# Weight rings whose four slots begin at different bytes modulo 256, in a decoder layer on one core

## Chip, cores and metric

The kernel runs on one core of a Trainium2 chip. The metric is the device time of one execution in microseconds (us); the median of three runs counts.

## What is computed

One step of a hybrid decoder layer for 264 tokens at once: 256 of a prompt and 8 samples, each with model width D = 2048. Everything is float32. Cut to its products, the reference is

```
z  = rms_norm(x) @ w_in                     # 2048 -> 3584: pool, lru, lru gate, conformer a, b
y_pool = pool_mixer(z_pool)  @ w_pool_br    # 512  -> 2048
y_lru  = (rg_lru(conv(z_lru)) * gelu(z_gate)) @ w_lru_br   # 1024 -> 2048
y_conf = silu(layer_norm(conv31(a * sigmoid(b)))) @ w_conf_br   # 512 -> 2048
gates  = sigmoid(rms_norm(x) @ w_gate + b_gate)            # 2048 -> 3 x 2048
x = x + (g_a * y_pool + g_b * y_lru + g_c * y_conf) @ w_out
x = x + square(relu(rms_norm(x) @ w_up)) @ w_down          # 2048 -> 8192 -> 2048
y = rms_norm(x)
```

The new recurrent states (the last rows of the convolutions and the pooling window, and the last h) are outputs too.

## The kernel before, in words

**Three matmuls for one product.** A float32 number is split into a high part, rounded to the type float32r, and a low part, the rest. For each tile of 128 x 128 weights `mm3` (lines 193 to 196) issues three matmuls: high weights by high x (L194), high weights by low x (L195), low weights by high x (L196). The weights are the operand that is loaded into the array; x is the moving operand, 264 columns wide (N = 264). So each matmul has a weight load of its own, which the profile lists as PEld.

**Chunks.** `weight_plan` cuts all weights into 478 chunks of 128 partitions x 1024 floats. A dense chunk holds two k-tiles (kt = 0, 1; 128 rows of the weight matrix each) of 512 output columns, so four tiles of 128 columns (m = 0 to 3) for each k-tile: 2 x 4 x 3 = 24 matmuls. A group is one block of 512 output columns: its chunks, numbered c, run over the rows of the matrix, and its four sums lie in four PSUM tiles. There are 472 dense chunks. Four chunks of lru gate weights stand between those of w_in, and behind chunk 3 of the first w_gate group stand one of group weights of the pooling ("grp") and an empty one. All the chunks are numbered i in the order of the work. Most groups have 8 chunks (16 k-tiles), those of w_lru_br 4, those of w_pool_br and w_conf_br 2.

**Rings.** Three rings of buffers carry the chunks. `raw` has NRAW = 6 slots of 1024 floats, filled by DMA from SyncE's queue (`dma_pair`, L138 for a pair of chunks in one transfer of 1 MB, or `dma_part`, L146 for one chunk). `split(j)` (L177, L178) turns a raw chunk into its two parts: ScalarE (ACT) casts to `whi`, VectorE (DVE) subtracts and writes `wlo`. These two have NHI = 4 slots; chunk j goes to slot j % 4. In the main loop, step i issues the split of chunk i + 3 (AHEAD), at even i the transfer of chunks i + 8 and i + 9, and then the matmuls of chunk i. Pairs from chunk SINGLE on are transferred as one.

**The moving operand.** Tiles of shape [128, ..., 264] in float32r hold x: `A` (high in k-tiles 0 to 15, low in 16 to 31), `xn` for w_up, `LH` and `Q` for the branches and the second half of the hidden layer, `L` for the lru gates. K-tile k of a chunk c is 2c + kt; one k-tile of x is 264 floats, 1056 bytes in each partition.

**Places in SBUF.** Tiles are placed one after the other in the order in which they are declared, behind the DMA scratch at byte 0 of each partition: raw, whi, wlo, qtmp, X, A, four tiles of 8 x 264 (tmp0 to tmp3, later xn), L, G, par, st, rstd, ones, ones_r and small ones. A tile that is declared later under the same tag takes the place of the earlier (Q that of qtmp, LH that of L). whi and wlo begin at byte 128 modulo 256.

**The other work.** Normalisation, convolutions, the scan, gates and splits of x run on ACT, DVE and GpSimd (POOL) between the splits, by a planner that has a budget for each engine and step (`run_bg`). At step 140 POOL issues the store of the states `st` (L973). Single matmuls with a tile of ones sum over the partitions for the norms (`ones_mm`, L271, and L992 at the end). The lru gates take twelve matmuls for one chunk, six for each of two k-tiles of L (`lru_gate_mm`).

The matmuls of one dense chunk are

```
for kt in range(2):
    for m in range(4):
        s = slice(kt * 512 + m * P, kt * 512 + (m + 1) * P)
        xh, xl = rhs(2 * c + kt)
        mm3(pss[m], whi[:, i % NHI, s], wlo[:, i % NHI, s], xh, xl, c == 0 and kt == 0, stop)
```

except for the first four chunks, where the three products go round the four m in turn, and the last two, where m is the outer loop.

Of the kernel before, what the change touches and what calls it, by code (L numbers as in the profile page):

```python
# [10 lines left out]
F32R = mybir.dt.float32r  # L11
# [4 lines left out]
P = 128  # L16
# [30 lines left out]
CH = 1024  # L47
NRAW = 6
NHI = 4
LRU_AT = ((4, 1), (4, 3), (4, 5), (4, 6))  # L50
WARM = 17
LEAD = 4
SINGLE = 18
AHEAD = 3


# [5 lines left out]
def weight_plan():  # L62
# [14 lines left out]
    for gi, (name, _, k, m) in enumerate(groups):  # L77
        for c in range(k // 2):
            chunks.append(("dense", gi, c, CH))
            if name == "w_in" and (m, c) in LRU_AT:  # L80
                chunks.append(("lru", LRU_AT.index((m, c)), 0, 512))
            if (name, m) == ("w_gate", 0) and c == 3:
# [5 lines left out]
def hybrid_step(ctx: ExitStack, tc: tile.TileContext, first, par_in, st_in, wall, y_out, st_out):  # L88
    nc = tc.nc
    cpool = ctx.enter_context(tc.tile_pool(name="cpool", bufs=1))  # L90
# [5 lines left out]


    raw = cpool.tile([P, NRAW, CH], F32, name="raw")
    whi = cpool.tile([P, NHI, CH], F32R, name="whi")
    wlo = cpool.tile([P, NHI, CH], F32R, name="wlo")  # L100
    qtmp = cpool.tile([P, 16 * N], F32, name="qtmp", tag="Q")
    X = cpool.tile([P, KD, N], F32, name="X")
    A = cpool.tile([P, 32, N], F32R, name="A")
# [4 lines left out]
    st = cpool.tile([P, S_OUT], F32, name="st")  # L108
# [7 lines left out]
    def pv(name, i=None, n=1):  # L116
        a, b = PCOL[name]
        return par[:, a:b] if i is None else par[:, a + i:a + i + n]

    def acc():  # L120
        return psum.tile([P, 512], F32, name="acc", tag="acc")
# [11 lines left out]
    def dma_pair(p):  # L133
        s = (2 * p) % NRAW
        if p >= n_pairs:
            return
        if 2 * p >= SINGLE and chunks[2 * p][3] == chunks[2 * p + 1][3] == CH:
            nc.sync.dma_start(raw[:, s:s + 2, :], wall[p - FIRST // 2].rearrange("p (a c) -> p a c", a=2))  # L138
        else:
            for h in range(2):  # L140
                if chunks[2 * p + h][3]:
                    dma_part(2 * p + h, 0, chunks[2 * p + h][3])
# [27 lines left out]
    def split(j, half=None):  # L170
        if j >= len(chunks) or not chunks[j][3]:
            return
        r, h, lo = raw[:, j % NRAW, :], whi[:, j % NHI, :], wlo[:, j % NHI, :]
        s = slice(0, chunks[j][3])
        if half is not None:
            s = slice(half * 512, half * 512 + 512)
        nc.scalar.copy(h[:, s], r[:, s])  # L177
        nc.vector.tensor_tensor(lo[:, s], r[:, s], f(h[:, s]), op=ALU.subtract)  # L178
# [133 lines left out]
    def x_tile(k):  # L312
        x_high(k)
        x_low(k)
# [31 lines left out]
    def softplus():  # L346
        sc = G[:, 8, :]
        t0, t1, t2, w, t4 = (sc[:, 8 * i:8 * i + 8] for i in range(5))
        lam = pv("lru_lambda")
        nc.scalar.activation(t0, lam, AF.Abs)  # L350
        nc.scalar.activation(w, t0, AF.Exp, scale=-1.0)
        nc.vector.tensor_scalar(t0, w, 2.0, None, op0=ALU.add)
        nc.vector.reciprocal(t1, t0)
        nc.vector.tensor_scalar(t4, lam, -1.0, 0.0, op0=ALU.mult, op1=ALU.max)
        eng = nc.gpsimd
        eng.tensor_tensor(t0, w, t1, op=ALU.mult)
        eng.tensor_tensor(t1, t0, t0, op=ALU.mult)
        terms = 10
        eng.memset(t2, 2.0 / (2 * terms + 1))
        for i in range(terms - 1, -1, -1):  # L360
            eng.tensor_tensor(t2, t2, t1, op=ALU.mult)
            eng.tensor_scalar(t2, t2, 1.0, 2.0 / (2 * i + 1), op0=ALU.mult, op1=ALU.add)
        eng.tensor_tensor(t2, t2, t0, op=ALU.mult)
        eng.tensor_tensor(t2, t2, t4, op=ALU.add)
        eng.tensor_scalar(sp[:, 0:8], t2, 4.0, 0.0, op0=ALU.mult, op1=ALU.add)
        eng.tensor_scalar(sp[:, 8:16], t2, -8.0, 0.0, op0=ALU.mult, op1=ALU.add)
# [89 lines left out]
    def lru_gate_mm(ct, c, j):  # L456
        assert "xc" in done
        hi, lo = whi[:, c % NHI, :], wlo[:, c % NHI, :]
        out = []
# [248 lines left out]
    def grp_mm(c):  # L708
        assert "pool" in done
        hi, lo = whi[:, c % NHI, :], wlo[:, c % NHI, :]  # L710
        for gi in range(4):
# [137 lines left out]
    def group(gi):  # L849
        name, k0, _, m = groups[gi]  # L850
        if name == "w_in":
            def rhs(i):
                return A[:, i, :], A[:, 16 + i, :]
            fn = {0: pool_evac, 1: lru_x_copy, 2: lambda c, p: lru_x_evac(4 + c, p), 3: gel_evac,
                  4: lambda c, p: gel_evac(4 + c, p), 5: ca_evac, 6: cb_evac}[m]
            return rhs, fn
        if name == "w_gate":
            return (lambda i: (A[:, i, :], A[:, 16 + i, :])), (lambda c, p: gate_evac(m // 4, m % 4, c, p))
        if name == "w_pool_br":
            assert "grp" in done  # L860
            return (lambda i: (Q(i), Q(8 + i))), (lambda c, p: branch_evac(0, m, c, p))
        if name == "w_lru_br":
            assert "lru" in done
            return (lambda i: (LH(i), LH(8 + i))), (lambda c, p: branch_evac(1, m, c, p))
        if name == "w_conf_br":
            assert "conf" in done
            return (lambda i: (Q(4 + i), Q(12 + i))), (lambda c, p: branch_evac(2, m, c, p))
        if name == "w_out":
            return (lambda i: (A[:, i, :], A[:, 16 + i, :])), (lambda c, p: out_evac(m * 4 + c, p))
        if name == "w_up":  # L870
            return bpart, (lambda c, p: up_evac(m // 4, (m % 4) * 4 + c, p))
        q = k0 // 16
        return (lambda i: hid(q, i)), (lambda c, p: down_evac(q, m * 4 + c, p))
# [23 lines left out]
    def by_operand(i, kt, rhs, pss):  # L897

        xh, xl = rhs(2 * i + kt)
        for k, (w, x) in enumerate(((whi, xh), (whi, xl), (wlo, xh))):  # L900
            for m in range(4):
                s = slice(kt * 512 + m * P, kt * 512 + (m + 1) * P)
                nc.tensor.matmul(pss[m][:, :N], w[:, i % NHI, s], x, start=i == kt == k == 0, stop=False)  # L903

    def tile_mm(i, c, kt, m, rhs, pss, stop):
# [3 lines that stand above are left out]
# [17 lines left out]
    for i, ch in enumerate(chunks):  # L926
        now[0] = i
        if i < 5:
            x_tile(2 * i + 6)
            x_tile(2 * i + 7)  # L930
        for half in (0, 1) if i < 2 else (None,):
            split(i + AHEAD, half)
        if i == 12:
            softplus()
            again = first[:, KD:KD + 4 * HEAD].rearrange("p (k c) -> p k c", k=4)[:, :, :N]
            nc.sync.dma_start(X[:, 0:4, :], again)
            nc.vector.tensor_scalar(gfin, pv("g_final"), -0.5, None, op0=ALU.mult)
        if i % 2 == 0:
            dma_pair((i + 8) // 2)
        if i == 2:  # L940
            nc.sync.dma_start(par, par_in)
            nc.sync.dma_start(st[:, :S_IN], st_in)
        kind, gi, c, _ = ch
        if kind == "dense":
            rhs, fn = group(gi)
            n = groups[gi][2] // 2
            if c == 0:
                pss = [acc() for _ in range(4)]
            if i < len(chunks) - 2:
                for kt in range(2):  # L950
                    if i < LEAD:
                        by_operand(i, kt, rhs, pss)
                    for m in range(4 * (i < LEAD), 4):
                        tile_mm(i, c, kt, m, rhs, pss, c == n - 1 and kt == 1)
            elif i == len(chunks) - 1:
                for m in range(4):
                    for b in range(4):
                        tile_mm(i - 1 + b // 2, c - 1 + b // 2, b % 2, m, rhs, pss, b == 3)
            if c == n - 1:
                for m in range(4):  # L960
                    fn(m, pss[m])
                after(gi)
        elif kind == "lru":
            for j in range(2):
                lru_gate_mm(2 * gi + j, i, j)
            if gi == 3:
                lru_tail()
        elif kind == "grp":
            grp_mm(i)
        if i == len(chunks) - 4:  # L970
            nc.scalar.preload_act_table_set(ROOT)
        if i == 140:
            nc.gpsimd.dma_start(st_out, st)  # L973
        if 5 <= i < 9:
            x_squares(i - 5)
        if i == 9:
            later(0, x_sum)
        if i == 12:
            later(0, x_rms)
        run_bg()  # L980
# [144 lines left out]
```

## Time and profile before

| what | value |
|---|---|
| median of three runs | 1404.62 us (1404.37 to 1404.83) |
| profiled execution | 1404.7 us |
| span of its instructions | 1402.9 us |
| matmuls, weight loads | 11,421 each |
| DMA | 257.49 MB, 184 GB/s in the mean |
| busy: DVE, ACT, POOL | 835.8, 722.3, 94.3 us |

The span runs from the first instruction of the program to the last. A timeline row gives the start from the beginning of the span, the duration, the engine ("SPq" is the queue of SyncE), the line of the kernel, the operation, output and inputs by their names, shapes, and the count of instructions that were merged into the row. The end of a matmul is modelled, and matmuls overlap in the pipeline; the distance of two starts is the measured quantity. A row of groups gives the count, the busy time and the mean duration, and then the idle time of the engine before them with what ended it. A row of waits gives the total, the number and the longest.

### The profile page before, as it was taken

The numbers are of one execution on the slowest core, as the hardware profiler recorded it, in microseconds if no ns is written. First come the engines' busy times: TensorE is split into PE (matmuls) and PEld (weight loads), VectorE is DVE, ScalarE is ACT, GpSimd is POOL, SyncE is SP. The second block draws the span as 40 slices with busy tenths as digits, with TensorE's granted clock in tenths as the row PEclk, the third lists the DMA queues.
The fourth block names the chain that finished last, engine by engine and source line by source line (L and its number), as shares of the span: only waits on it lengthen the run. The fifth ranks groups of instructions, "written<-read, shape, count | busy, mean of one in ns | idle before, by whom it ended". The sixth has DMA issues, their size and how long they took to land.

```text
span 1402.9 us, 26642 instructions
## 1 busy us (share of the span) xinstructions
PE 1392.3 (99%) x11421; PEld 1390.5 (99%) x11421; DVE 835.8 (60%) x1052; ACT 722.3 (51%) x1021; POOL 94.3 (7%) x123
## 2 busy tenths in 40 slices
PE   9999999999999999999999999999999999999997
PEld 9999999999999999999999999999999999999997
DVE  8685787766766658565545444554455544455544
ACT  7757576656664645455544334543344533354544
POOL 0220010110102013010000000000000000000012
PEclk9999999999999999999999999999999999999999
DMA  9555555555655554555555555555555555555551
GB/s 363 170 173 188 185 185 191 181 182 181 210 182 180 179 182 160 202 177 172 192 181 181 180 182 180 181 180 182 179 182 178 183 179 182 181 181 179 180 183 74
DMA packets 39814, 257.49 MB, mean 184 GB/s; under 512 B 4368, under 2 KB 5520, under 8 KB 10896
## 3 DMA queue, kind: packets, MB, share of 16 engines
q1 hardware_dynamic: 39120, 254.15, 53.2%
q8 instruction: 89, 1.46, 0.4%
q0 software_dynamic: 144, 1.04, 0.2%
q10 hardware_dynamic: 432, 0.61, 0.1%
q14 instruction: 29, 0.24, 0.1%
HBM read 252.57 MB, written 3.21 MB: 182 GB/s over the span
## 4 chain that ended last, share of the span: by engine, by line
PE 99%; DVE 0%; DMA 0%; ACT 0%; DVEq 0%; issue 0%
PE acc L196 33%; PE acc L194 33%; PE acc L195 33%; PE acc L903 1%; DMA tmp<-first_dram 0%; DVE y L1014 0%; DVE acc L1005 0%; DVEq L1104 0%; DVE G L1004 0%; DVE acc L1003 0%; PE acc L992 0%; PE acc L271 0%; ACT whi L187 0%; ACT rstd L998 0%; DVE G L834 0%
## 5 line engine op out<-in xcount | busy, mean ns | idle before, releaser
L178 DVE TENSOR_TENSOR wlo<-raw,whi 128x1024 fp32r<-128x1024 f32 (+1 forms) x478 | 584.1, 1224 | 541.8 <-ACT whi L177 541.0
L177 ACT CAST whi<-raw 128x1024 fp32r<-128x1024 f32 (+1 forms) x478 | 495.3, 1039 | 614.2 <-PE acc L195 560.2
L194 PE MATMUL acc<-A,whi 128*128 128x264 f32 x1952 | 556.0, 285 | 0.0
L196 PE MATMUL acc<-A,wlo 128*128 128x264 f32 x1952 | 555.2, 284 | 0.0
L195 PE MATMUL acc<-A,whi 128*128 128x264 f32 x1952 | 554.3, 284 | 0.0
L195 PEld LDWEIGHTS acc<-A,whi 128*128 128x128 f32 x1952 | 368.8, 189 | 0.0
L196 PEld LDWEIGHTS acc<-A,wlo 128*128 128x128 f32 x1952 | 368.1, 189 | 0.0
L194 PEld LDWEIGHTS acc<-A,whi 128*128 128x128 f32 x1952 | 367.9, 188 | 0.0
L194 PE MATMUL acc<-xn,whi 128*128 128x264 f32 x1024 | 291.7, 285 | 0.0
L196 PE MATMUL acc<-xn,wlo 128*128 128x264 f32 x1024 | 291.3, 284 | 0.0
L195 PE MATMUL acc<-xn,whi 128*128 128x264 f32 x1024 | 290.8, 284 | 0.0
L195 PEld LDWEIGHTS acc<-xn,whi 128*128 128x128 f32 x1024 | 193.5, 189 | 0.0
L196 PEld LDWEIGHTS acc<-xn,wlo 128*128 128x128 f32 x1024 | 193.1, 189 | 0.0
L194 PEld LDWEIGHTS acc<-xn,whi 128*128 128x128 f32 x1024 | 193.0, 188 | 0.0
L195 PE MATMUL acc<-Q,whi 128*128 128x264 f32 x644 | 182.9, 284 | 0.0
L194 PE MATMUL acc<-LH,whi 128*128 128x264 f32 x640 | 182.3, 285 | 0.0
L196 PE MATMUL acc<-LH,wlo 128*128 128x264 f32 x640 | 182.0, 284 | 0.0
L195 PEld LDWEIGHTS acc<-Q,whi 128*128 128x128 f32 x644 | 121.7, 189 | 0.0
L196 PEld LDWEIGHTS acc<-LH,wlo 128*128 128x128 f32 x640 | 120.7, 189 | 0.0
L194 PEld LDWEIGHTS acc<-LH,whi 128*128 128x128 f32 x640 | 120.6, 188 | 0.0
L804 POOL TENSOR_TENSOR G<-G 128x264 f32<-128x264 f32 x28 | 25.7, 919 | 809.1 <-ACT G L802 808.2
L585 ACT ACTIVATE G<-tmp,par 128x256 f32<-128x256 f32 x120 | 54.3, 500 | 1.3 <-DVE G L599 0.7
(195 smaller groups left out, 792.5 us busy)
## 6 DMA issues: line engine op xcount, KB each, us to landing
raw<-wall_dram SPq DMA_DIRECT2D x225, 1024.0 KB, 4.9
raw<-wall_dram SPq DMA_DIRECT2D x14, 512.0 KB, 7.2
raw<-first_dram SPq DMA_DIRECT2D x6, 512.0 KB, 8.0
X<-first_dram SPq DMA_DIRECT2D x6, 264.0 KB, 7.8
raw<-wall_dram SPq DMA_DIRECT2D x5, 256.0 KB, 2.9
tmp<-first_dram SPq DMA_DIRECT2D x3, 388.0 KB, 5.1
so_dram<-st POOLq DMA_DIRECT2D x1, 1018.0 KB, 5.7
st<-st_dram SPq DMA_DIRECT2D x1, 912.0 KB, 8.8
```

What stands on the lines that cost most here:

```text
L177: nc.scalar.copy(h[:, s], r[:, s])
L178: nc.vector.tensor_tensor(lo[:, s], r[:, s], f(h[:, s]), op=ALU.subtract)
L194: nc.tensor.matmul(ps[:, :N], whi_t, xh, start=first, stop=False)
L195: nc.tensor.matmul(ps[:, :N], whi_t, xl, start=False, stop=False)
L196: nc.tensor.matmul(ps[:, :N], wlo_t, xh, start=False, stop=last)
L585: nc.scalar.activation(dst[:, ct, :TP], vext[:, ct, k:k + TP], AF.Copy, scale=par[:, w:w + 1])
L804: nc.gpsimd.tensor_tensor(sq2, sq2, t, op=ALU.add)
L903: nc.tensor.matmul(pss[m][:, :N], w[:, i % NHI, s], x, start=i == kt == k == 0, stop=False)
```

## The change

```
 NHI = 4
+STEP = CH + 16
+SHIFT = 0
...
-SINGLE = 18
+SINGLE = 16
...
-    whi = cpool.tile([P, NHI, CH], F32R, name="whi")
-    wlo = cpool.tile([P, NHI, CH], F32R, name="wlo")
+    whi = cpool.tile([P, SHIFT + NHI * STEP], F32R, name="whi")[:, SHIFT:SHIFT + NHI * STEP].rearrange("p (a c) -> p a c", a=NHI)
+    wlo = cpool.tile([P, SHIFT + NHI * STEP], F32R, name="wlo")[:, SHIFT:SHIFT + NHI * STEP].rearrange("p (a c) -> p a c", a=NHI)
...
         if i == 140:
-            nc.gpsimd.dma_start(st_out, st)
+            nc.sync.dma_start(st_out, st)
...
-    nc = _bacc.Bacc("TRN2", target_bir_lowering=False, num_devices=1)
+    nc = _bacc.Bacc("TRN2", target_bir_lowering=False, num_devices=1, dynamic_dma_scratch_size=8192)
```

The slots of whi and wlo lie 1040 floats (4160 bytes) apart instead of 1024 (4096), so slots 0 to 3 begin at 128, 192, 0 and 64 modulo 256. Each ring grows by 256 bytes in a partition, and all tiles behind it move by that much. The scratch for DMA descriptors shrinks to 8192 bytes. The states are stored by SyncE's queue instead of POOL's. The pair of chunks 16 and 17 is transferred at once and no longer one by one.

## Prediction

> **What bounds the kernel now.** I read the page first: the busy table, the granted clock and the chain that ended last.
>
> ```profile
> span 1402.9 us, 26642 instructions
> PE 1392.3 (99%) x11421; PEld 1390.5 (99%) x11421; DVE 835.8 (60%) x1052; ACT 722.3 (51%) x1021; POOL 94.3 (7%) x123
> PEclk9999999999999999999999999999999999999999
> PE 99%; DVE 0%; DMA 0%; ACT 0%; DVEq 0%; issue 0%
> ```
>
> TensorE (PE) is busy for the whole span at full clock, the chain consists of matmuls, and no other engine passes 60%. A busy PE says only that matmuls follow one another without a hole. Their spacing sets the time: 1392.3 us / 11,421 = 121.9 ns from one start to the next. So I asked next whether this spacing has slack in it. The timeline at the very end of the kernel shows matmuls of line 992, of another form, and the timeline of one group of w_out shows the ordinary ones:
>
> ```profile
> 1391.47 0.61 PE L992 MATMUL acc<-G,ones 128*128 128x132 f32 x4
> ...
> 573.33 0.28 PE L194 MATMUL acc<-A,whi 128*128 128x264 f32 x1
> 576.25 0.29 PE L194 MATMUL acc<-A,whi 128*128 128x264 f32 x1
> 579.16 0.29 PE L194 MATMUL acc<-A,whi 128*128 128x264 f32 x1
> 580.64 0.29 PE L194 MATMUL acc<-A,whi 128*128 128x264 f32 x1
> 582.11 0.28 PE L194 MATMUL acc<-A,whi 128*128 128x264 f32 x1
> 585.02 0.28 PE L194 MATMUL acc<-A,whi 128*128 128x264 f32 x1
> ```
>
> Four matmuls of line 992 end 0.61 us after the first starts; with 0.28 us for one, three spacings take 0.33 us, 0.11 us each. Ordinary matmuls take 0.122. The other rows are the first matmuls of chunks 0, 1, 2, 3 and 4 of the second w_out group (found by counting matmuls in program order, 24 to a chunk); 580.64 is where chunk 2 goes over to its second k-tile. The four chunks take 2.92, 2.91, 2.95 and 2.91 us. They hold the same 24 matmuls of the same sizes, and nothing waits. What differs is where the moving operand begins. Its k-tiles are N = 264 floats, 1056 bytes, apart; 1056 = 4 x 256 + 32, so k-tile number k begins at 128 + 32k modulo 256 (raw, whi, wlo, qtmp and X before it are whole multiples of 256 bytes, and all begin at 128). The weights begin at 128 for every slot, k-tile and m. Call the distance weight minus moving d: it is -32k modulo 256, and runs through all eight values in four chunks. The chunk with k = 4, 5 (d = 128 and 96) is the slow one: 1.48 us for its first k-tile, 1.47 for its second.
>
> The cycle is 11.69 us, 2.9225 per chunk, and it stands for the kernel: from 573.33 to 1391.47 there are 280 chunks, 818.14 / 280 = 2.922 us.
>
> The Trainium skill, "SBUF — State Buffer", section "Who interferes with whom", gives PE two independent read ports and says that PE never waits on anyone. By that rule the four chunks would be equal, and the change would do nothing (the last rival below). Rows that differ by 40 ns between equal chunks speak against it.
>
> **The change, part by part.**
>
> *The rings.* STEP = 1040 floats puts slot s at 128 + 64s. Slot and chunk advance together, and the moving operand advances 64 bytes per chunk, so d stops turning: it is 64(i - c) - 32kt, for chunk number i with index c in its group. Six chunks that are not dense (four lru, grp, none) make i - c congruent to 2 modulo 4 (the two-chunk groups of w_pool_br and w_conf_br turn it to 0 and back) for all 288 chunks of w_out, w_up and w_down and for 86 others: 374 chunks have d = 128 in the first k-tile and 96 in the second, the pair of the slow chunk. 95 have i - c congruent to 0, so d = 0 and -32, the pair of the 2.92 chunk; 3 are odd. (All 472 dense chunks are counted.)
>
> Taken row by row, 374 chunks would go from 2.9225 to 2.95: 374 x 0.0275 = +10.3 us. But the rows show that the distance alone doesn't set the pace: what ran just before does too. These are starts of chunks with the same residues, each followed by the start of what comes next, after other neighbours:
>
> ```profile
> 105.91 0.28 PE L194 MATMUL acc<-A,whi 128*128 128x264 f32 x1
> 108.81 0.28 PE L194 MATMUL acc<-A,whi 128*128 128x264 f32 x1
> 120.46 0.29 PE L194 MATMUL acc<-A,whi 128*128 128x264 f32 x1
> 123.38 0.28 PE L194 MATMUL acc<-L,whi 128*128 128x264 f32 x1
> 526.54 0.28 PE L194 MATMUL acc<-Q,whi 128*128 128x264 f32 x1
> 529.49 0.28 PE L194 MATMUL acc<-Q,whi 128*128 128x264 f32 x1
> 660.97 0.28 PE L271 MATMUL acc<-LH,ones_r 128*128 128x264 f32 x1
> 661.09 0.28 PE L194 MATMUL acc<-xn,whi 128*128 128x264 f32 x1
> 663.99 0.28 PE L194 MATMUL acc<-xn,whi 128*128 128x264 f32 x1
> 251.86 0.29 PE L194 MATMUL acc<-LH,whi 128*128 128x264 f32 x1
> 254.76 0.28 PE L194 MATMUL acc<-LH,whi 128*128 128x264 f32 x1
> ```
>
> The first four pairs all have k = 4, 5. After the matmul on ones_r (line 271) the pair takes 2.90 us; after the lru gate matmuls of slots 0 and 1 (105.91) 2.90; after those of slots 4 and 5 (120.46) 2.92; after k = 6, 7 (w_conf_br, 526.54) 2.95; and after k = 2, 3 (the regular case) 2.95. So at d = 128 there are two paces, and the entry chooses. The last pair, k = 0, 1 at the start of w_lru_br, takes 2.90 where the regular one takes 2.92.
>
> After the change each such chunk is entered from a k-tile at d = 96, again and again, and the pace that the first entry finds will repeat in all. The nearest row is 120.46: before it come six lru gate matmuls on L's index 5, which are at d = 96 too. It is not the same entry: during the last matmul of a chunk the first weights of the next slot are loaded, and these will lie 64 bytes further (d = 160 for that one load); the regular slow chunk has this 160 as well. So both ends stay: 2.90 to 2.95. I take the fast pace, half-way between the nearest row (2.92) and the other two (2.90): 2.91, 374 x (2.91 - 2.9225) = -4.7 us. For the 95 chunks at d = 0 and -32 I take 2.91, between 2.90 and 2.92: -1.2 us.
>
> *SINGLE 16.* Chunks 16 and 17 come by one transfer instead of two. It must wait for both slots, so for chunk 11's split:
>
> ```profile
> 30.26 1.22 DVE L178 TENSOR_TENSOR wlo<-raw,whi 128x1024 fp32r<-128x1024 f32 x1
> 44.11 1.04 ACT L177 CAST whi<-raw 128x1024 fp32r<-128x1024 f32 x1
> raw<-wall_dram SPq DMA_DIRECT2D x225, 1024.0 KB, 4.9
> so_dram<-st POOLq DMA_DIRECT2D x1, 1018.0 KB, 5.7
> ```
>
> That split ends at 31.48; with 4.9 us to landing the data are there at 36.5, and chunk 16 is cast at 44.11. 7 us to spare: nothing.
>
> *The states' store.* SyncE's issue order gains one store after the weights of chunks 148 and 149:
>
> ```profile
> L518 POOL COPY st<-tmp x1: 193/193/193, 189.8 to 189.8; 128x8 f32<-128x8 f32 x1
> 373.43 0.74 POOL L973 DMA_DIRECT2D so_dram<-st  x1
> 371.20 17.73 SPq L138 DMA_DIRECT2D raw<-wall_dram  x4
> SPq L138 <- DVE wlo L178: 1205.0, 223, 9.6
> ACT whi L177 <- PE acc L195: 560.2, 351, 3.7
> ```
>
> The last writer of st ends at 190 us, the store is issued after 371, so SyncE doesn't wait in front of it. Queued behind it is the next weight transfer. The four transfers issued within 17.73 us are one per two chunks, because each waits for a split to free the slot. If the store held the queue for all of its 5.7 us, the next transfer would start that much later at worst; it is cast five chunks (14.6 us) after its slot is freed and lands 4.9 us after its issue, which leaves 9.7 us. That covers 5.7; without the cover it would cost up to 5.7 us once. ACT's cast waits for PE, not for data, so the cover is real. POOL's 0.74 us goes from an engine that is 7% busy: nothing.
>
> *Scratch 8 KB.* It makes room for the 512 bytes; no POOL transfer is left to use it, and a shift by 8192 - 512 bytes leaves every residue. Nothing. The splits write the same lengths to other residues; DVE and ACT have 40% and 49% free.
>
> **The sum.** -4.7 - 1.2 = -5.9 us: the span goes from 1402.9 to 1397.0. The profiled execution took 1404.7, 1.8 us around its span, and the median of the runs is 1404.62, so both give the same: 1398.7 us.
>
> **The rivals.**
>
> *The slow pace at d = 128 (slower).* The entry d = 96, 160, 128 leads where the regular one, 128 after 160, leads. For it: the regular chunks and w_conf_br, and the load at 160. Against: three other entries, among them the one from d = 96. Price 374 x 0.0275 = +10.3 us less 0.2 for the others: 1414.7. It decides at the third matmul or so of the first such chunk, and then holds in all 374.
>
> *Weight residue alone.* Line 992's 0.11 us has weights in the tile ones, whose bytes (by the sizes of par, st and rstd, each rounded up to 32) begin at 64 modulo 256, the residue of slot 3. If loads from there were free of the loss, a quarter of 11,328 matmuls would gain 0.012 us each: -34 us, 1371. Against: ones_r begins at 64 as well, and the matmuls around 660.97 keep 0.12 us; line 992 differs in form. [...]
>
> *Nothing changes.* Only the moving operand's own residue counts, or no address does: the eight residues still come equally often, 1404.6. For it: only the moving residue varies in this trace, so its effect and that of d can't be told apart here. Against: spacing that depends on what was loaded before means that loads and streaming meet.
>
> **Chances and range.** Fast pace 0.50, slow pace 0.35, nothing 0.12, residue alone 0.03. The fast pace's own range runs from 2.90 for all (374 x 0.0225 + 95 x 0.0225 = -10.6, 1394.1) to 2.92 for all (-1.1, 1403.5). A measurement tells about 0.2%, 2.8 us, from no change; 0.05 of the fast case lies within that. Faster 0.45 + 0.03 = 0.48, within 0.2% 0.12 + 0.05 = 0.17, slower 0.35. The range reaches into the slow case: 1395 to 1415.5.
>
> **What would show it.** In the changed kernel the four chunks of a w_out group last the same; if they alternate as now, the distance is not what counts. Their length is 2.90 to 2.92 (forecast) or 2.95 (first rival). The first k-tile of a chunk takes about 1.44 us (2.91 less the 1.47 of the second) at the fast pace, 1.48 at the slow. Casts still wait for PE; a gap before a matmul near 380 us would show the store's cover gone.

## The result, and the profile after

The changed kernel takes 1413.44 us in the median of three runs (1413.06 to 1413.62), against 1404.62: the ratio is 1.0061, with a 95% interval of 1.0043 to 1.0079. The forecast, 1398.7, was on the wrong side; the range held the time, and the first rival (1414.7) was close to it.

The page of the changed kernel begins like the one before; the span and PE's busy time have both grown by 8.4 us.

```profile
span 1411.3 us, 26639 instructions
PE 1400.7 (99%) x11421; PEld 1399.2 (99%) x11421; DVE 836.4 (59%) x1052; ACT 721.9 (51%) x1021; POOL 93.6 (7%) x122
PE 99%; DVE 0%; DMA 0%; ACT 0%; DVEq 0%; issue 0%
```

So the time is in the spacing of the matmuls again. Here is the timeline at the first matmuls of the same five chunks of the second w_out group (start in us first), with the second k-tile of chunk 2 at 581.75:

```profile
574.37 0.29 PE L196 MATMUL acc<-A,whi 128*128 128x264 f32 x1
577.32 0.29 PE L196 MATMUL acc<-A,whi 128*128 128x264 f32 x1
580.26 0.29 PE L196 MATMUL acc<-A,whi 128*128 128x264 f32 x1
581.75 0.29 PE L196 MATMUL acc<-A,whi 128*128 128x264 f32 x1
583.21 0.29 PE L196 MATMUL acc<-A,whi 128*128 128x264 f32 x1
586.16 0.29 PE L196 MATMUL acc<-A,whi 128*128 128x264 f32 x1
```

2.92, 2.91, 2.95 and 2.91 have become four times 2.95 to the rounding (11.79 us for four, 2.948 each). The first k-tile takes 1.49 us, the second 1.46: distance 128 at the slow pace. And one chunk of the same kernel shows that the pace is not in the distances alone. It follows a matmul on ones_r in the first w_up group:

```profile
662.82 0.28 PE L273 MATMUL acc<-LH,ones_r 128*128 128x264 f32 x1
662.94 0.28 PE L196 MATMUL acc<-xn,whi 128*128 128x264 f32 x1
665.85 0.29 PE L196 MATMUL acc<-xn,whi 128*128 128x264 f32 x1
668.79 0.29 PE L196 MATMUL acc<-xn,whi 128*128 128x264 f32 x1
```

2.91 for it, and 2.94 by these rounded starts (2.949 in the trace) for the next, which is entered in the regular way again (from a k-tile at distance 96, through the load at 160). The chunks of the first w_gate group behind the group weights show the same: the first matmuls of its chunk 4, of that chunk's second k-tile, and of chunks 5 and 6.

```profile
186.73 0.28 PE L196 MATMUL acc<-A,whi 128*128 128x264 f32 x1
188.17 0.28 PE L196 MATMUL acc<-A,whi 128*128 128x264 f32 x1
189.63 0.29 PE L196 MATMUL acc<-A,whi 128*128 128x264 f32 x1
192.58 0.29 PE L196 MATMUL acc<-A,whi 128*128 128x264 f32 x1
```

2.90 us, with 1.44 for the k-tile at distance 128, and then 2.95. Counted over the trace, nine of the 374 chunks are entered in another way: seven take 2.90 to 2.925 us and two, behind a matmul on ones_r, 2.94. Of the 363 entered in the regular way, 361 take 2.94 to 2.95 (the last two chunks of the kernel have another order and are left out). The other two stand right behind the two that took 2.94. Here is the first of them, the chunk that begins at 447.74:

```profile
444.68 0.28 PE L273 MATMUL acc<-Q,ones_r 128*128 128x264 f32 x1
444.80 0.29 PE L196 MATMUL acc<-A,whi 128*128 128x264 f32 x1
447.74 0.28 PE L196 MATMUL acc<-A,whi 128*128 128x264 f32 x1
450.64 0.29 PE L196 MATMUL acc<-A,whi 128*128 128x264 f32 x1
453.59 0.29 PE L196 MATMUL acc<-A,whi 128*128 128x264 f32 x1
```

2.94, 2.90, 2.95. So the regular entry makes the slow pace anew at each chunk, but what ran earlier than the last k-tile can count too.

The sum agrees: by the starts of the matmuls in both traces the 374 chunks take 9.7 us more than before, and the 95 at distances 0 and -32, which run mostly at 2.92 or 2.90 in turn, 1.1 us less. Together that is +8.6, with 8.4 measured.

### The profile page after: what moved, and what is told of

Read it like the earlier page. It is cut to its first block, busy times and chain, and to the rows that moved or that the text cites. A ratio compares the mean times of both kernels' runs of the same rounds, so it can differ in the third digit from the quotient of the medians.

```text
span 1411.3 us, 26639 instructions
## 1 busy us (share of the span) xinstructions
PE 1400.7 (99%) x11421; PEld 1399.2 (99%) x11421; DVE 836.4 (59%) x1052; ACT 721.9 (51%) x1021; POOL 93.6 (7%) x122
## 3 DMA queue, kind: packets, MB, share of 16 engines
q8 instruction: 89, 1.46, 0.4%
## 4 chain that ended last, share of the span: by engine, by line
PE 99%; DVE 0%; DMA 0%; ACT 0%; DVEq 0%; issue 0%
PE acc L196 33%; PE acc L197 33%; PE acc L198 33%; PE acc L905 1%; DMA tmp<-first_dram 0%; DVE y L1016 0%; DVE acc L1007 0%; DVEq L1106 0%; DVE G L1006 0%; DVE acc L1005 0%; PE acc L994 0%; PE acc L273 0%; ACT whi L189 0%; ACT rstd L1000 0%; DVE G L836 0%
```

## Experiments

**Only the stride undone.**

```
-STEP = CH + 16
+STEP = CH
```

> Everything of the change except the stride: slots 4096 bytes apart again, with the 8 KB scratch, the store of the states on SyncE and chunks 16 and 17 in one transfer. Theory A (the distance d between the first bytes of weights and moving operand modulo 256, together with what was loaded just before, sets the spacing of the matmuls): the chunks of a w_out group go back to 2.92, 2.91, 2.95 and 2.91 us and the time to 1404.6. Rival B (the store, the scratch or the transfer costs the 8.8 us): 1413, or part of the way there.

1404.62 us; ratio to before 0.9999 (0.9989 to 1.0009). The timeline at the same chunks:

```profile
573.15 0.28 PE L196 MATMUL acc<-A,whi 128*128 128x264 f32 x1
576.07 0.29 PE L196 MATMUL acc<-A,whi 128*128 128x264 f32 x1
578.98 0.29 PE L196 MATMUL acc<-A,whi 128*128 128x264 f32 x1
581.92 0.28 PE L196 MATMUL acc<-A,whi 128*128 128x264 f32 x1
584.84 0.28 PE L196 MATMUL acc<-A,whi 128*128 128x264 f32 x1
```

2.92, 2.91, 2.94 and 2.92: the old cycle (to the rounding of the starts). Rival B is out: the store, the scratch and the single transfer cost nothing that can be measured, and all 8.8 us belong to the stride.

**All tiles 64 bytes further.**

```
+    cpool.tile([P, 16], F32, name="pad")
     raw = cpool.tile([P, NRAW, CH], F32, name="raw")
```

> The changed kernel with 64 bytes of padding ahead of the first tile: every tile begins 64 bytes further, so all distances stay and all residues change. Theory A: chunks of 2.95 us throughout w_out, w_up and w_down, 1413.4. Rival C (the absolute residue of weights or of the moving operand counts, for instance the weights at 0 and 64): chunks of different lengths, and a time that is off by 2 us or more.

1413.21 us, ratio 1.006 (1.0045 to 1.0075).

```profile
574.67 0.29 PE L197 MATMUL acc<-A,whi 128*128 128x264 f32 x1
577.62 0.29 PE L197 MATMUL acc<-A,whi 128*128 128x264 f32 x1
580.57 0.29 PE L197 MATMUL acc<-A,whi 128*128 128x264 f32 x1
583.52 0.29 PE L197 MATMUL acc<-A,whi 128*128 128x264 f32 x1
```

2.95 each. Every chunk has other residues of weights and moving operand, and nothing changes: it is the distance that counts, not the place. This is shown for steps of 64 bytes alone. It adds little to the changed kernel, whose four slots lie 64 bytes apart modulo 256: each slot takes here the residues that the next slot had there.

**Scans of the distance.** In these four kernels the rings are moved by o bytes more for each group from w_out on, so one run shows sixteen distances; pieces of the rings are wide enough for it. The core of the edit (`shift` in floats; KT = 512 in the first scan, 520 in the others; in scan_lo only wlo is shifted, and scan_fine leaves out the factor 4):

```
+    def shift(j, t):
+        g = chunks[j][1] if chunks[j][0] == "dense" else 0
+        return 4 * (max(g - 31, 0) % 16)
+    def slot(t, j):
+        at = j % NHI * STEP + shift(j, t)
+        return t[:, at:at + 2 * KT].rearrange("p (k c) -> p k c", k=2)[:, :, :512]
```

> The changed kernel with the rings moved by 16 bytes more for each group from w_out on: sixteen steps, so that the first and second k-tile lie at distances 128 + o and 96 + o. Each group has eight chunks, so its pace can be read. Theory A, from the rows of the kernel before: 2.95 us a chunk at o = 0, 2.905 at o = 64 (the regular chunk 1 of before), 2.90 to 2.92 at o = 128 (chunk 0), 2.91 at o = 192 (chunk 3); values between them at the other steps, unknown at odd multiples of 16. Rival C: 2.95 at every step, or no order by o. The sum over the groups would come to about 2.92 in the mean, 1405.

> As the scan before, but the second k-tile of a chunk begins 32 bytes further in the rings too, so that both k-tiles of all chunks of a group lie at one distance, 128 + o. Theory A: one pace for each o; from the k-tiles of the kernel before, once settled, 1.44 or 1.48 us a k-tile at d = 128, 1.46 at 96, 1.44 at 32 (2.88 a chunk, the lowest). If what comes just before counts too, the same o can give two paces. Rival C: no order by o.

> Both k-tiles at distance 128 for the high weights; the ring of the low weights moved by 16 bytes more for each group from w_out on, so that every third load lies at another distance. Theory A: 2.882 us at o = 0, other values at other steps, none below 2.88 if that is the floor of two loads that a stream overtakes; a lower one would show that the floor is no floor. Rival C (only the high weights or the moving operand count): 2.882 at every step.

> Both k-tiles at distance 128 + o with o rising by 4 bytes for each group from w_out on, sixteen steps from 0 to 60. Theory A with 16 bytes as the smallest unit: the values of the scan in steps of 16 (2.882, 2.928, 2.91 to 2.95, 2.882 at 0, 16, 32 and 48) hold for four steps each, or weights that begin inside a unit cost something more in the three steps between. No theory gives a figure there.

In scan_two, where o falls back from 240 to 0, a slot overwrites the last 44 columns of its neighbour, so the weights of a few tiles there are not the right ones; the instructions are the same. Microseconds for one chunk in the settled part of a group (start of its chunk 7 less that of chunk 2, divided by 5), by o:

| o, bytes | 0 | 16 | 32 | 48 | 64 | 80 | 96 | 112 |
|---|---|---|---|---|---|---|---|---|
| scan_two (128 + o, 96 + o) | 2.948 | 2.915 | 3.008 | 2.888 | 2.935 | 2.908 | 2.915 | 2.895 |
| scan_one (128 + o, both) | 2.882 | 2.928 | 2.933 | 2.882 | 2.908 | 2.918 | 2.922 | 2.908 |
| scan_lo (low weights alone) | 2.882 | 2.942 | 2.911 | 2.882 | 2.915 | 2.922 | 2.975 | 2.928 |

| o, bytes | 128 | 144 | 160 | 176 | 192 | 208 | 224 | 240 |
|---|---|---|---|---|---|---|---|---|
| scan_two | 2.906 | 2.882 | 2.882 | 2.882 | 2.907 | 2.882 | 2.955 | 2.902 |
| scan_one | 2.922 | 2.919 | 2.882 | 2.882 | 2.922 | 2.935 | 2.923 | 2.908 |
| scan_lo | 2.915 | 2.942 | 2.895 | 2.908 | 2.935 | 2.922 | 2.908 | 2.922 |

Each o comes at least twice, in different matrices and with different moving tiles, and the second visit gives the same figure to a nanosecond or two (the table shows the second, since the first w_up group holds a matmul on ones_r and differs there by up to 0.024). scan_fine gave, from o = 0 to 60 in steps of 4: 2.882, 2.895, 2.888, 2.922, 2.928, 2.902, 2.928, 2.922, 2.932, 2.895, 2.895, 2.939, 2.882, 2.882, 2.888, 2.894.

Four pairs of starts from which the figures come: scan_one at o = 0 and at 16, scan_two at o = 32, scan_lo at o = 96 (chunks 2 and 7 of each group).

```profile
552.72 0.28 PE L205 MATMUL acc<-A,whi 128*128 128x264 f32 x1
567.13 0.28 PE L205 MATMUL acc<-A,whi 128*128 128x264 f32 x1
...
575.88 0.28 PE L205 MATMUL acc<-A,whi 128*128 128x264 f32 x1
590.52 0.28 PE L205 MATMUL acc<-A,whi 128*128 128x264 f32 x1
```

```profile
604.50 0.29 PE L205 MATMUL acc<-A,whi 128*128 128x264 f32 x1
619.54 0.29 PE L205 MATMUL acc<-A,whi 128*128 128x264 f32 x1
```

```profile
692.99 0.29 PE L205 MATMUL acc<-xn,whi 128*128 128x264 f32 x1
707.86 0.29 PE L205 MATMUL acc<-xn,whi 128*128 128x264 f32 x1
```

14.41, 14.64, 15.04 and 14.87 us for five chunks of equal work. The whole kernels took 1405.16 us (scan_two), 1398.77 (scan_one), 1400.96 (scan_lo) and 1396.88 (scan_fine), one run each. What follows: only the weights were moved here, so the moving operand's own residue is not the cause (rival C is out); the low weights count by themselves; a step of 4 bytes already changes the pace, so the expected unit of 16 bytes does not hold; and no settled pace is under 2.88 us (120.1 ns a matmul), though many distances reach it.

The rows of the kernel before foretold part of this. In scan_two, 2.95 was expected at o = 0, 2.90 to 2.92 at 128 and 2.91 at 192, and 2.948, 2.906 and 2.907 came, as did the mean of about 1405 us; at 64 it should have been 2.905 and was 2.935, and the steps between ran from 2.882 to 3.008 instead of lying between these values. In scan_one all three distances for which a figure was expected gave it: 2.882 at 128 (o = 0), 2.923 at 96 (o = 224) and 2.882 at 32 (o = 160). The miss at 64 shows that a k-tile's pace does not always carry over from one order of distances to another.

**The two k-tiles in the other order.**

```
-                for kt in range(2):
+                for kt in (0, 1) if i < LEAD else (1, 0):
...
-                        for m in range(4 * (i < LEAD), 4):
-                            tile_mm(i, c, kt, m, rhs, pss, c == n - 1 and kt == 1)
+                        for m in range(4 * (i < LEAD), 4):
+                            tile_mm(i, c, kt, m, rhs, pss, c == n - 1 and kt == 0)
```

(and the sum is opened by kt = 1 of chunk 0.)

> The changed kernel with the two k-tiles of each chunk taken in the other order, from chunk 4 on: same tiles, same distances of 128 and 96, but the k-tile at 128 is now entered from 96 without the load at 160 (that border now lies at 192, ahead of the k-tile at 96). Theory A with the entry through 160 as the cause of the slow pace: 2.90 to 2.92 us a chunk, about 1399. Rival D (distance 128 after 96 is slow whatever is loaded between): 2.95, 1413.

1396.61 us in one run, with 1404.59 for the kernel before on the same chip. The starts of chunk 1 of the second w_out group, of the k-tile that it now takes second (kt = 0, at distance 128) and of the next chunk:

```profile
573.67 0.28 PE L196 MATMUL acc<-A,whi 128*128 128x264 f32 x1
575.13 0.28 PE L196 MATMUL acc<-A,whi 128*128 128x264 f32 x1
576.57 0.28 PE L196 MATMUL acc<-A,whi 128*128 128x264 f32 x1
```

1.46 us at 96 and 1.44 at 128, 2.90 in all. The same tiles at the same distances run 0.05 us a chunk faster than in the changed kernel. What differs is the borders: the k-tile at 128 comes straight after 96, and the one at 96 after 128 through a load at 192. The first is the entry of the row at 120.46 in the kernel before, and it is fast here too. Rival D is out. Both borders changed in this run, so it shows that the borders decide, and not which part of them.

**All chunks at distance 128.**

```
+KT = 520
+STEP = 1104
...
+        return 32 if chunks[j][0] == "dense" and (j - chunks[j][2]) % 4 == 0 else 0
```

> Second k-tile 32 bytes further in the rings, and the slots of the groups with i - c congruent to 0 moved by 128 bytes, so that all dense chunks lie at distance 128 in both k-tiles. Theory A (distance and entry): the fast pace of the scan's o = 0, 2.882 us a chunk, everywhere: 1404.6 - 472 x (2.922 - 2.882) = 1385.7. Rival D (distance 128 is slow by itself, and the scan's fast groups owe it to their neighbours): 2.95 a chunk, 1415 to 1418.

1386.81 us (1386.65 to 1387.06), ratio to before 0.9872 (0.9856 to 0.9889): 17.8 us less than before, 26.6 less than the changed kernel, and the fastest of all here. Its page and the same chunks:

```profile
span 1385.3 us, 26639 instructions
PE 1374.9 (99%) x11421; PEld 1373.2 (99%) x11421; DVE 836.4 (60%) x1052; ACT 721.6 (52%) x1021; POOL 93.5 (7%) x122
```

```profile
566.90 0.28 PE L205 MATMUL acc<-A,whi 128*128 128x264 f32 x1
569.78 0.28 PE L205 MATMUL acc<-A,whi 128*128 128x264 f32 x1
572.66 0.28 PE L205 MATMUL acc<-A,whi 128*128 128x264 f32 x1
575.54 0.28 PE L205 MATMUL acc<-A,whi 128*128 128x264 f32 x1
578.43 0.28 PE L205 MATMUL acc<-A,whi 128*128 128x264 f32 x1
```

2.88 for each. Distance 128, at which the changed kernel is slow, gives here the shortest settled time that any run showed. Rival D is out here too. Every k-tile of this kernel is entered through a load at 160 as well, so the load at 160 alone does not make the slow pace: coming from 96 through 160 goes with it in 361 of 363 chunks of the changed kernel, and coming from 128 through 160 does not.

## Why the prediction was wrong, point by point

- **What bounds the kernel**: right. PE's spacing is the time; the distance of weights and moving operand modulo 256 and what ran before set it. No_stride, the scans and swap_k show it. The Trainium skill ("SBUF — State Buffer", section "Who interferes with whom") calls the two read ports of PE independent. The conclusion that the prediction drew from it, equal chunks in equal time, does not hold in these runs: chunks of equal work take from 2.88 to 3.01 us.
- **Two paces at distance 128**: right, and shown: the changed kernel (2.948) and swap_k (2.90) hold the same k-tiles. That what ran before chooses between them is shown as well.
- **The step that failed** is "I take the fast pace, half-way between the nearest row (2.92) and the other two (2.90)". The term was -4.7 us and came to +9.7. Two things in it were wrong. First, "the pace that the first entry finds will repeat in all": seven of the nine chunks with another entry found a faster pace (2.90 at 186.73), and it did not repeat; the next chunk was slow, and so was nearly every one that was entered in the regular way. Second, the row for this regular entry. The nearest row was chosen by the distance before the border, 96, and the text itself named what it lacked: the one load at 160. The regular slow chunk of the kernel before has that load, and its pace (2.95) is the one that came; swap_k, which has the entry of the row at 120.46 and not that load, is fast like that row.
- **The 95 chunks at 0 and -32**: 2.91 forecast, mostly 2.92 and 2.90 in turn; the mean, 2.91, was right (-1.1 us for -1.2).
- **SINGLE, scratch, store**: nothing, as forecast. One detail was off. SyncE issues the store at 406.51, not soon after 371, since that queue first issues the weights of chunks 148 and 149, which wait for their slots, while POOL had run ahead; and it takes 9.3 us to land, not 5.7. The timeline of its queue, and its row among the DMA issues (count, KB, us to landing):

```profile
400.32 6.14 SPq L140 DMA_DIRECT2D raw<-wall_dram  x2
406.51 0.42 SPq L975 DMA_DIRECT2D so_dram<-st  x1
411.95 6.14 SPq L140 DMA_DIRECT2D raw<-wall_dram  x2
```

```profile
so_dram<-st SPq DMA_DIRECT2D x1, 1018.0 KB, 9.3
```

  The issue of weights goes on behind it every two chunks, and the profile shows no wait of PE between 400 and 425 us.
- **The rivals**: the slow pace came, 1.3 us under its price: the 374 chunks cost 9.7 us where it had 10.3, and the 95 gained 1.1 where it had 0.2. That the range held the time is owed to this rival, to which the range had been stretched, and not to the forecast. Its reason, that the pace is found once and then holds in all, failed with the forecast's. Weight residue alone is out by the four equal chunks of the changed kernel, one of whose slots begins at 64. "Nothing changes" is out by the result.

Open: what inside PE or its reads makes several paces at one distance, how far back the memory reaches (the two fast chunks behind the matmuls on ones_r at 444.68 and later), and where the 120.1 ns come from, when line 992's matmuls, of another form, follow one another in 0.11 us. The runs show that the paces repeat to a nanosecond or two, not by what mechanism.

## What to carry to other kernels

Where one engine is busy for the whole span, compare the spacing of its instructions over equal pieces of work: a cycle in it (here 2.92, 2.91, 2.95, 2.91) points to a cost that no busy time shows. When the pace depends on what ran before, a row carries over only with its whole neighbourhood, every load at the border included, and an entry that comes at every piece of work weighs more than the first one. Such a setting is found by a scan, and one run can hold sixteen settings if they are given to sixteen groups.

## What was not expected of the hardware

At fixed work, moving the weights by 4 bytes changes the spacing of float32r matmuls (2.882 to 2.895 us for 24); with the k-tiles at two distances 32 bytes apart it reached 3.008; and moving the low weights alone changes it from 2.882 to 2.975. A settled pace was never under 2.88, and the same 2.882 came at many settings: a floor of 120.1 ns a matmul in these runs.
